# A hybrid attention and convolution block: one more large buffer and two fewer small ones, convolution operands in pairs of token halves, and earlier loads for the attention merges

## The chip, the cores and the metric

The kernel runs on one core of a Trainium2 chip. The metric is the device time of one execution in microseconds (us); the figure given for a kernel is the median of its timed runs. Beside that there is one profiled execution, whose trace gives the time of every instruction and of every DMA.

## The reference, cut to what matters

The block takes x (1024 tokens, 1024 channels), and everything is float32. A matrix product is made on TensorE from high and low parts (`hi*a + hi*b + lo*a`), so each product costs three matmuls, and each operand has first to be split by ScalarE (the high part) and VectorE or GpSimd (the low part).

```python
h = rms_norm(x, g_pre_mix)
q, k, v, glu_in, z_ga, z_gc = split(h @ w_in)
# three head groups, dilation 1, 4 and 16; each gives an output o_g and a log denominator lse_g
alpha  = softmax(stack(lse_g), axis=groups)
y_attn = (sum_g alpha_g * o_g) @ w_attn_out              # the "merge", then "ao"
u      = depthwise_conv(u * sigmoid(gate)) + b_dw
y_conv = silu(layer_norm(u)) @ w_conv_out + b_conv_out    # "co"
merged = sigmoid(z_ga) * y_attn + sigmoid(z_gc) * y_conv
x = x + rms_norm(merged @ w_mix_out)                      # then the SwiGLU FFN
```

## The kernel before

The engines' instruction streams are written out by hand: each engine executes its instructions in the order in which the Python code emits them. Two clocks in that code set the order. `unit()` emits one product of 128 channels by 512 tokens: for each of 8 k-tiles three matmuls, then a `tick()`. A tick runs the steps that `later(n, step)` has put n ticks ahead, one piece of a weight split at every third tick, and one step of each background generator in `gens` (a generator that yields n skips n ticks). After each matmul, `beat()` advances the attention generator by `RATE` steps, so attention is woven into whatever product is running.

The stages that matter here, in order:

1. The value products `B.v(g, hg)` run with `conv_norm` in the background: it normalizes the convolution's output and, in its last loop, lets VectorE multiply (L1272) and ScalarE apply Silu (L1276), block after block. In the kernel before, ScalarE writes the result with even and odd tokens brought into their natural places (a stride of two elements) and itself starts the store to DRAM (L1278).
2. Attention starts in the second of these products and goes on through the rest of them, through `plain_gate` (the late gate) and the first products of the convolution's output projection. For each head pair and group it loads queries and keys by `stack_load` (L872 to L879, DMAs of 64 rows each), the bias tile (L483) and the values (L900 to L905). `att_s` makes the scores, `att_e` the exponentials (L1066), `att_t` transposes them (L1091, split at L1098 and L1099), and `att_p` multiplies by the values (L1126) and copies the result to an output tile (L1145) that is stored in `d_att`. A step's `att_t` comes three steps after its exponentials, its `att_p` one step after its `att_t`.
3. `conv_split` loads the Silu results from `d_act` half a block at a time (L1292) and splits them (L1222 on ScalarE, L1223 on VectorE) into the operands of the projection.
4. The projection runs over (n, hf) in the order (0,0), (1,0), (0,1), (1,1), (2,0), (2,1) and so on; n is the column of weights `co[n]` (loaded at L177, split at L188 and L189) and hf the half of the tokens. VectorE takes a finished product out of PSUM and multiplies it by its gate (L1557); gates are loaded at L1540 and stored at L1559.
5. `merge(hp)` combines the three groups of a head pair: it computes the weights alpha in a small tile (L1170 to L1177), writes them to `d_w` (L1180), and, after attention has ended (`self.fine is None`) and its turn has come, loads each group's output (L1190) and its weights spread over 64 partitions twice (`spread`, L1158), multiplies and adds on VectorE (L1197, L1201, L1205, L1209, L1212), and splits the result. The merges of head pairs 0 and 1 have their weights ready long before attention ends.

All DMAs but the Silu stores, and a few at the start, are started by SyncE (SP) and go to one queue. Large buffers (`slot`, 128 x 1024) number 41, small ones (`half`, 128 x 512) 13; PSUM in the attention stage is divided into two banks each for products (`g`), scores (`s`), transposes (`t`) and outputs (`o`), and is divided anew for products (`g=6, s=2`) once attention has ended.

Of the kernel before, what the change touches and what calls it, by code (L numbers as in the profile page):

```python
# [46 lines left out]
NSLOT = 41  # L47

NRING = 3
NHALF = 13  # L50
# [12 lines left out]
class Build:  # L63
# [135 lines left out]
    def quarters(self, i, c):  # L199


        nc = self.nc
        if c == 0:
            self.hl[i] = {}
        o = self.hl[i]
        r1, r2 = self.raw[i - 1], self.raw[i]
        a11, a12, a21, a22 = r1[:, :H], r1[:, H:], r2[:, :H], r2[:, H:]
        add = self.wsplit.tensor_tensor
        l, r = slice(0, H), slice(H, 2 * H)
        if c == 0:  # L210
            h, w = self.both(r1)
            o["A11"], o["A12"] = (h[:, l], w[:, l]), (h[:, r], w[:, r])
        elif c == 1:
            self.s12 = self.ring()
            add(self.s12[:, l], a21, a22, op=OP.add)
            add(self.s12[:, r], self.s12[:, l], a11, op=OP.add)  # L216
        elif c == 2:
            h, w = self.both(self.s12)
            o["S1"], o["S2"] = (h[:, l], w[:, l]), (h[:, r], w[:, r])
        elif c == 3:  # L220
            self.s34 = self.half(), self.half()
            add(self.s34[0], a11, a21, op=OP.add)
            add(self.s34[1], self.s12[:, r], a12, op=OP.add)
            self.s12 = None
        elif c == 4:
            h, w = self.slot(F32R), self.slot(F32R)
            for n, s in ("S3", l), ("S4", r):
                x = self.s34[n == "S4"]
                nc.scalar.copy(h[:, s], x)
                add(w[:, s], x, f(h[:, s]), op=OP.subtract)  # L230
                o[n] = (h[:, s], w[:, s])
            self.s34 = x = None
        else:
            x, y = self.half(F32R), self.half(F32R)
            nc.scalar.copy(x, a22)
            add(y, a22, f(x), op=OP.subtract)
            o["A22"] = (x, y)
            del self.raw[i], self.raw[i - 1], self.hl[i]
# [863 lines left out]
    def att_p(self, live, k):  # L1102
# [33 lines left out]
        O = self.O  # L1136
        if g == 0:
            d = O[:, u * 128:u * 128 + 256]
        elif g == 1:
            d = O.rearrange("p (t c) -> p c t", c=4)[:, u // 2]  # L1140
        else:
            d = O.rearrange("p (m c) -> p c m", c=8)[:, u:u + 2]
        for h in range(2):
            x = ps[0:64, h * 256:(h + 1) * 256]
            nc.vector.tensor_copy(d[h * 64:(h + 1) * 64], x if g < 2 else x.rearrange("p (c m) -> p c m", c=2))  # L1145
# [16 lines left out]
    def merge(self, hp, st):  # L1162
# [33 lines left out]
        yield 8  # L1196
        nc.vector.tensor_tensor(y, y, x, op=OP.mult)  # L1197
# [14 lines left out]
        nc.vector.tensor_tensor(y, y, w, op=OP.add)  # L1212
        w = None
        yield 2
        self.OT[hp] = self.both(y)

    turn = 0
# [12 lines left out]
    def conv_norm(self):  # L1230
# [39 lines left out]
        for b in range(9):  # L1270
            if b < 8:
                nc.vector.tensor_tensor(A[b], A[b], rs, op=OP.mult)  # L1272
            if b:
                a, A[b - 1] = A[b - 1], None
                o = self.slot()
                nc.scalar.activation(o.rearrange("p (m e) -> p e m", e=2), a.rearrange("p (e m) -> p e m", e=2),  # L1276
                                     AF.Silu, bias=self.col(C_BLN + b - 1), scale=self.col(C_GLN + b - 1))
                nc.scalar.dma_start(self.d_act[b - 1], o)  # L1278
# [6 lines left out]
    def conv_split(self):  # L1285
        self.cop = [[], []]
        nc = self.nc

        def load(i):
            hf, b = divmod(i, 8)  # L1290
            x = self.half()
            nc.sync.dma_start(x, self.d_act[b][:, hf * H:(hf + 1) * H])  # L1292
# [82 lines left out]
def build(ctx, tc, aps):  # L1375
# [81 lines left out]
    def plain_gate(n, job, early):  # L1457
        w = B.weights(job)
# [12 lines left out]
        if not early:  # L1471
            nc.sync.dma_start(B.d_gc[n], s)
# [39 lines left out]
    for i, (g, hg) in enumerate(vj):  # L1512
# [15 lines left out]
    def conv_rhs(hf):  # L1528
        def at(kt):
            while len(B.cop[hf]) <= kt:  # L1530
                next(cs[0])
# [6 lines left out]
    def gate_load(d):  # L1538
        c = B.slot()
        nc.sync.dma_start(c, d)  # L1540
# [21 lines left out]
    B.finish(cs)  # L1562
# [443 lines left out]
```

## Time and profile before

| | us |
|---|---|
| median of 3 runs | 1735.37 |
| lowest, highest run | 1732.92, 1735.95 |
| profiled execution, its own time | 1730.98 |
| its span in the trace | 1729.2 |

The profiled execution took 1.8 us more than its span, and 4.4 us less than the median. The trace has 24623 instructions; the granted TensorE clock was 0.996 on average. In what follows PE is TensorE, PEld its weight loads, DVE VectorE, ACT ScalarE, POOL GpSimd and SP SyncE; a q behind an engine's name means its sequencer, such as a DMA start. Times of day are us from the start of the span.

### The profile page before, as it was taken

The numbers are of one execution on the slowest core, as the hardware profiler recorded it, in microseconds if no ns is written. First come the engines' busy times: TensorE is split into PE (matmuls) and PEld (weight loads), VectorE is DVE, ScalarE is ACT, GpSimd is POOL, SyncE is SP. The second block draws the span as 40 slices with busy tenths as digits, with TensorE's granted clock in tenths as the row PEclk, the third lists the DMA queues.
The fourth block names the chain that finished last, engine by engine and source line by source line (L and its number), as shares of the span: only waits on it lengthen the run. The fifth ranks groups of instructions, "written<-read, shape, count | busy, mean of one in ns | idle before, by whom it ended". The sixth has DMA issues, their size and how long they took to land.

```text
span 1729.2 us, 24623 instructions
## 1 busy us (share of the span) xinstructions
PE 1698.1 (98%) x8754; PEld 1441.0 (83%) x8754; DVE 1255.7 (73%) x2235; ACT 793.6 (46%) x1589; POOL 466.9 (27%) x387
## 2 busy tenths in 40 slices
PE   8999999999999989999998999999999999999998
PEld 7788888888888989999886888888888888888786
DVE  6789978888997566777955855676556655677586
ACT  6344444344444476676612345743333333354463
POOL 0017778887885233433200120000000000000000
PEclk9999999999999999999999999999999999999999
DMA  4352434455678697879699731223322322494234
GB/s 164 109 175 87 158 116 141 163 180 168 183 181 217 183 282 206 243 200 229 208 278 322 268 129 62 104 74 122 116 91 92 121 99 92 149 372 148 84 136 153
DMA packets 170872, 285.53 MB, mean 165 GB/s; under 512 B 55506, under 2 KB 86733, under 8 KB 170749
## 3 DMA queue, kind: packets, MB, share of 16 engines
q1 hardware_dynamic: 169196, 279.26, 51.1%
q10 hardware_dynamic: 1440, 4.46, 0.7%
q8 instruction: 69, 1.13, 0.3%
q14 instruction: 55, 0.44, 0.1%
q0 software_dynamic: 112, 0.24, 0.0%
HBM read 192.15 MB, written 96.47 MB: 167 GB/s over the span
## 4 chain that ended last, share of the span: by engine, by line
PE 89%; DMA 5%; ACT 2%; DVE 2%; issue 1%; SPq 1%; POOL 0%; ACTq 0%; DVEq 0%; POOLq 0%
PE p L326 16%; PE p L325 16%; PE p L327 16%; PE p L1890 12%; PE p L1619 4%; PE p L309 3%; PE p L311 3%; PE p L313 3%; PE p L1126 3%; PE p L1053 2%; PE p L950 2%; PE p L952 2%; PE p L954 2%; PE p L560 2%; DMA b<-dw 2%; PE p L1091 2%
## 5 line engine op out<-in xcount | busy, mean ns | idle before, releaser
L325 PE MATMUL p<-b,b 128*128 128x512 f32 x1032 | 401.6, 389 | 0.0
L327 PE MATMUL p<-b,b 128*128 128x512 f32 x1032 | 401.5, 389 | 0.0
L326 PE MATMUL p<-b,b 128*128 128x512 f32 x1032 | 401.5, 389 | 0.0
L325 PEld LDWEIGHTS p<-b,b 128*128 128x128 f32 x1032 | 193.7, 188 | 41.1 <-ACT c L339 0.6
L327 PEld LDWEIGHTS p<-b,b 128*128 128x128 f32 x1032 | 193.7, 188 | 40.1
L326 PEld LDWEIGHTS p<-b,b 128*128 128x128 f32 x1032 | 193.7, 188 | 40.1
L1890 PE MATMUL p<-b,b 128*128 128x512 f32 x924 | 210.2, 389 | 0.9 <-ACT b L1222 0.7
L1890 PEld LDWEIGHTS p<-b,b 128*128 128x128 f32 x924 | 173.4, 188 | 37.6 <-ACT b L1222 1.1
L690 DVE SCALAR_TENSOR_TENSOR p<-b,par,p 128x511 f32<-128x511 f32 (+14 forms) x232 | 163.3, 738 | 0.0
L313 PE MATMUL p<-b,b 128*128 128x512 f32 x368 | 147.1, 400 | 9.1 <-DVE b L189 9.1
L309 PE MATMUL p<-b,b 128*128 128x512 f32 x368 | 147.5, 401 | 0.0
L311 PE MATMUL p<-b,b 128*128 128x512 f32 x368 | 146.6, 398 | 0.0
L195 ACT CAST b<-d 128x1024 fp32r<-128x1024 f32 x86 | 90.4, 1051 | 108.3 <-POOL d L216 58.2
L196 POOL TENSOR_TENSOR b<-d,b 128x1024 fp32r<-128x1024 f32 x44 | 106.9, 2429 | 101.6 <-ACT b L195 88.5
L196 DVE TENSOR_TENSOR b<-d,b 128x1024 fp32r<-128x1024 f32 x42 | 51.3, 1221 | 105.1 <-ACT b L195 105.1
L950 PE MATMUL p<-b,b 128*128 128x256 f32 x384 | 113.4, 295 | 2.4 <-ACT d L965 2.4
L954 PE MATMUL p<-b,b 128*128 128x256 f32 x384 | 112.5, 293 | 0.0
L952 PE MATMUL p<-b,b 128*128 128x256 f32 x384 | 112.4, 293 | 0.0
L1223 DVE TENSOR_TENSOR b<-c,b 128x512 fp32r<-128x512 f32 x101 | 70.9, 702 | 41.6 <-ACT b L1222 40.8
L1222 ACT CAST b<-c 128x512 fp32r<-128x512 f32 x101 | 62.5, 618 | 67.2 <-PE p L1890 22.5
L1223 DVE TENSOR_TENSOR b<-b,b 128x512 fp32r<-128x512 f32 x117 | 79.9, 687 | 18.3 <-ACT b L1222 16.6
L1066 ACT ACTIVATE c<-c,stat 128x128 f32<-128x128 f32 (+1 forms) x192 | 84.9, 445 | 12.3 <-DVE stat L1056 11.6
(234 smaller groups left out, 3349.5 us busy)
## 6 DMA issues: line engine op xcount, KB each, us to landing
b<-w_in SPq DMA_DIRECT2D x30, 512.0 KB, 5.2
dk<-c SPq DMA_DIRECT2D x48, 256.0 KB, 2.9
dq<-c SPq DMA_DIRECT2D x48, 256.0 KB, 3.6
b<-dq SPq DMA_DIRECT2D x48, 256.0 KB, 4.7
b<-dk SPq DMA_DIRECT2D x48, 256.0 KB, 6.7
b<-w_fi SPq DMA_DIRECT2D x24, 512.0 KB, 4.9
d<-w_in SPq DMA_DIRECT2D x23, 512.0 KB, 4.5
dqS<-c SPq DMA_DIRECT2D x44, 256.0 KB, 2.1
```

The source lines that it names most:

```text
L196: self.wsplit.tensor_tensor(lo, x, f(hi), op=OP.subtract)
L309: nc.tensor.matmul(ps, hi[:, s], a, start=kt == 0, stop=False)
L311: nc.tensor.matmul(ps, hi[:, s], b, start=False, stop=False)
L313: nc.tensor.matmul(ps, lo[:, s], a, start=False, stop=kt == nk - 1)
L325: nc.tensor.matmul(ps, hi[:, s], a, start=first and kt == 0, stop=False, skip_group_check=True)
L326: nc.tensor.matmul(ps, hi[:, s], b, start=False, stop=False, skip_group_check=True)
L327: nc.tensor.matmul(ps, lo[:, s], a, start=False, stop=kt == 3, skip_group_check=True)
L690: nc.vector.scalar_tensor_tensor(A[i][:, j:], src[i][:, :H - j], w[i], A[i][:, j:], op0=OP.mult, op1=OP.add)
L950: nc.tensor.matmul(o, a, hi[:, s], start=kt == 0, stop=False)
L954: nc.tensor.matmul(o, b, hi[:, s], start=False, stop=kt == KT - 1)
L1223: nc.vector.tensor_tensor(s[:, 512:512 + n], src, f(s[:, :n]), op=OP.subtract)
L1890: nc.tensor.matmul(acc[t], x, y, start=first and e == 0, stop=last and e == 2, skip_group_check=True)
```

## The change

- **Buffers.** `NSLOT` 41 becomes 42, `NHALF` 13 becomes 11. In `quarters`, which prepares weights for the products by seven multiplications, the sums S3 and S4 and the split of A22 move from two small buffers each to one large one each, and the split of S3 and S4 is one instruction each on ScalarE and GpSimd instead of two.
- **Convolution operands.** `conv_norm` writes the Silu results with even tokens first and odd tokens behind, without a stride, and their stores are started by SP five ticks later instead of by ScalarE at once. `conv_split` loads two halves into one large buffer, keeps two pairs, starts 16 ticks later than before, and splits with other gaps. The half hf of the projection is now the even or the odd tokens, and the gate is read and written with a stride of two.
- **Merges.** The attention outputs are laid out so that alpha can be written to `d_w` in rows of 128 numbers (six rows of 8 x 128 tokens): the weights go through a transpose on TensorE and a copy on ScalarE first. A merge may load its first two groups as soon as the projection has begun (`self.hH is None`) and it is at most one turn ahead; only its multiplications wait for the end of attention. PSUM is divided anew once all four merges have their weights (`weighed == 4`).
- **DMAs put off.** The store of an attention output comes three ticks after its last copy instead of one; the late gate's store, the first gate load and the first column of projection weights are issued some ticks later, the second column with the first product of the projection.

The core of the diff:

```diff
-NSLOT = 41
+NSLOT = 42
-NHALF = 13
+NHALF = 11
...
         elif c == 4:
-            h, w = self.slot(F32R), self.slot(F32R)
-            for n, s in ("S3", l), ("S4", r):
...
+            h, w = self.both(self.s34)
+            o["S3"], o["S4"] = (h[:, l], w[:, l]), (h[:, r], w[:, r])
...
-            x, y = self.half(F32R), self.half(F32R)
+            x = self.slot(F32R)
...
-            self.later(1, lambda x=self.O: nc.sync.dma_start(self.d_att[g, hp], x))
+            self.later(3, lambda x=self.O: nc.sync.dma_start(self.d_att[g, hp], x))
...
         yield 1
-        nc.sync.dma_start(self.d_w[hp].rearrange("f (p u) -> p f u", u=8),
-                          t[:, 80:].rearrange("p (f u) -> p f u", u=8))
-        t = m = r = w = low = tot = None
-        yield 6
-
-        while self.fine is not None or hp > self.turn:
+        m = r = w = low = tot = None
+        yield 3
+        ps = self.bank("t")
+        nc.tensor.transpose(ps[0:48, :128], t[:, 80:], self.ident)
+        nc.scalar.copy(t[0:48], ps[0:48, :128])
+        ps = None
+        self.weighed += 1
+        yield 1
+        nc.sync.dma_start(self.d_w[hp].rearrange("f (u p) -> (f u) p", u=8), t[0:48])
+        t = None
+        yield 4
+
+        while self.hH is not None or hp > self.turn + 1:
             yield 0
...
         z, w = load(1), self.spread(hp, 1)
         yield 8
+        while self.fine is not None or hp > self.turn:
+            yield 0
         nc.vector.tensor_tensor(y, y, x, op=OP.mult)
...
-                nc.scalar.activation(o.rearrange("p (m e) -> p e m", e=2), a.rearrange("p (e m) -> p e m", e=2),
-                                     AF.Silu, bias=self.col(C_BLN + b - 1), scale=self.col(C_GLN + b - 1))
-                nc.scalar.dma_start(self.d_act[b - 1], o)
+                nc.scalar.activation(o, a, AF.Silu, bias=self.col(C_BLN + b - 1), scale=self.col(C_GLN + b - 1))
+                self.later(5, lambda b=b, o=o: nc.sync.dma_start(self.d_act[b - 1], o))
...
-        x = [load(i) for i in range(3)]
-        yield 14
+        self.cn = 0
+        x = [load(), load()]
+        yield 16
         for i in range(16):
-            self.cop[i // 8].append(self.split(x.pop(0), H))
-            if i < 13:
-                x.append(load(i + 3))
-            yield 3 if i < 3 else 1 + i % 2
-            while i == 3 and not self.room:
+            while i > 3 and not self.room:
                 yield 0
+            self.cop[i // 8].append(self.split(x[0][:, i % 2 * H:(i % 2 + 1) * H], H))
+            if i % 2:
+                x.pop(0)
+                if self.cn < 16:
+                    x.append(load())
+            yield 2 if i < 4 else 1 + i % 2
...
-        w = B.weights(job)
+        w = B.weights(job) if early else B.timed([job], co[:1], 3, 9)[0]
...
-            nc.sync.dma_start(B.d_gc[n], s)
+            B.later(4, lambda: nc.sync.dma_start(B.d_gc[n], s))
...
-            cs = B.bg(B.conv_split())
-            B.later(20, lambda: B.load_ahead(co[0]))
+            cs = []
+            B.later(16, lambda: cs.append(B.bg(B.conv_split())))
...
-    nxt = gate_load(B.d_gc[0])
+    nxt = gate_load(B.d_gc[0], 3)
...
-        if B.tags["g"] == 2 and B.fine is None:
+        if B.tags["g"] == 2 and B.weighed == 4:
             B.banks(g=6, s=2)
         ps = B.unit(ws[n], conv_rhs(hf), KT)
-        c = mg[n][:, hf * H:(hf + 1) * H]
+        c = mg[n].rearrange("p (m e) -> p e m", e=2)[:, hf]
```

More of the change, by code (lines that the diff above doesn't have):

```diff
@@ L220, in quarters @@
         elif c == 3:
[L221 to L223 removed]
+            self.s34 = self.slot()
+            add(self.s34[:, l], a11, a21, op=OP.add)
+            add(self.s34[:, r], self.s12[:, r], a12, op=OP.add)
             self.s12 = None
         elif c == 4:
[L226 to L237 removed]
+            h, w = self.both(self.s34)
+            o["S3"], o["S4"] = (h[:, l], w[:, l]), (h[:, r], w[:, r])
+            self.s34 = None
+        else:
+            x = self.slot(F32R)
+            nc.scalar.copy(x[:, l], a22)
+            add(x[:, r], a22, f(x[:, l]), op=OP.subtract)
+            o["A22"] = (x[:, l], x[:, r])
             del self.raw[i], self.raw[i - 1], self.hl[i]
@@ L1211, in merge @@
         yield 2
-        nc.vector.tensor_tensor(y, y, w, op=OP.add)
-        w = None
+        z = self.slot()
+        nc.vector.tensor_tensor(z.rearrange("p (m c) -> p c m", c=8), *(a.rearrange("p (c m) -> p c m", c=8) for a in (y, w)),
+                                op=OP.add)
+        y = w = None
         yield 2
-        self.OT[hp] = self.both(y)
-    turn = 0
+        self.OT[hp] = self.both(z)
+    turn = weighed = 0
     def split(self, src, n):
@@ L1275, in conv_norm @@
                 o = self.slot()
[L1276 to L1278 removed]
+                nc.scalar.activation(o, a, AF.Silu, bias=self.col(C_BLN + b - 1), scale=self.col(C_GLN + b - 1))
+                self.later(5, lambda b=b, o=o: nc.sync.dma_start(self.d_act[b - 1], o))
+                o = None
             yield 1
@@ L1287, in conv_split, with load @@
         nc = self.nc
[L1289 to L1292, printed above, removed]
-            return x
-        x = [load(i) for i in range(3)]
-        yield 14
+        def load():
+            x = self.slot()
+            for e in range(2):
+                hf, b = divmod(self.cn + e, 8)
+                nc.sync.dma_start(x[:, e * H:(e + 1) * H], self.d_act[b][:, hf * H:(hf + 1) * H])
+            self.cn += 2
+            return x
+        self.cn = 0
+        x = [load(), load()]
+        yield 16
         for i in range(16):
-            self.cop[i // 8].append(self.split(x.pop(0), H))
-            if i < 13:
-                x.append(load(i + 3))
-            yield 3 if i < 3 else 1 + i % 2
-            while i == 3 and not self.room:
-                yield 0
+            while i > 3 and not self.room:
+                yield 0
+            self.cop[i // 8].append(self.split(x[0][:, i % 2 * H:(i % 2 + 1) * H], H))
[4 more added lines that the diff above has]
+            yield 2 if i < 4 else 1 + i % 2
     def rstd_rows(self, m, e):
@@ L1536, in build, with gate_load @@
     mg = {}
-    def gate_load(d):
+    def gate_load(d, late=0):
         c = B.slot()
-        nc.sync.dma_start(c, d)
+        if late:
+            B.later(late, lambda: nc.sync.dma_start(c, d))
+        else:
+            nc.sync.dma_start(c, d)
         return c
-    nxt = gate_load(B.d_gc[0])
+    nxt = gate_load(B.d_gc[0], 3)
     ws = {}
```

13 lines of the change are left out of this document (7 added, 6 removed).

## The prediction

> **What bounds the kernel now.** I read the page first, then TensorE's waits, then a table by stages.
>
> ```profile
> PE 1698.1 (98%) x8754; PEld 1441.0 (83%) x8754; DVE 1255.7 (73%) x2235; ACT 793.6 (46%) x1589; POOL 466.9 (27%) x387
> ```
>
> PE is busy for 98% of the span, so a change that leaves the products alone can only win the places where PE waits. The list of its waits (us in total, times, longest) names them:
>
> ```profile
> PE p L313 <- DVE b L189: 9.1, 3, 4.8
> ...
> PE p L950 <- ACT d L965: 2.4, 2, 1.5
> PE p L1053 <- DVE stat L1056: 2.4, 1, 2.4
> PE p L1053 <- DMA b<-dk: 1.3, 1, 1.3
> ```
>
> Three places: about 600 to 620, where ScalarE is late (4.8 us); one wait for keys (1.3); and the projection, where PE waits for a weight split on VectorE (9.1). The stage table (stretch, length, busy of PE, PEld, DVE, ACT and POOL, granted clock, DMA share, GB/s) shows the last of them and what the DMA engines do before it:
>
> ```profile
> 600.00:620.00 20.00, 15.22 (x123) 14.61 (x122) 13.13 (x16) 15.23 (x15) 9.37 (x7) 1.00 0.73 269
> 820.00:847.00 27.00, 25.70 (x188) 21.82 (x187) 23.80 (x74) 20.33 (x70) 9.64 (x13) 1.00 1.02 315
> 847.00:868.00 21.00, 20.63 (x145) 16.70 (x144) 18.48 (x53) 10.38 (x37) 2.77 (x4) 1.00 0.14 43
> 868.00:902.00 34.00, 33.70 (x149) 27.57 (x147) 18.54 (x26) 4.10 (x7) 0.00 (x0) 1.00 1.00 304
> 902.00:940.00 38.00, 29.19 (x113) 23.27 (x114) 23.89 (x26) 8.02 (x12) 0.00 (x0) 0.91 1.03 320
> ```
>
> The DMA queue is full from 820 to 847 (share 1.02), idle for 21 us (0.14) while attention ends, and full again while the merges run. From 902 on the waits also lower the clock to 0.91, which costs 38 x 0.09 = 3.4 us. So the projection loses 9.1 + 3.4 = 12.5 us. The change moves four of the merges' twelve group loads, with their weights, in front of that idle stretch.
>
> **Part 1, the Silu stores (600 to 620).** ScalarE's timeline (start, length, operation, idle time before it):
>
> ```profile
> 610.46 1.34 ACT L1276 ACTIVATE b<-b,par 128x1024 f32<-128x1024 f32 x1 [0.46 <-ACT b L1276]
> 611.83 0.33 ACTq L1278 DMA_DIRECT2D dact<-b  x1
> 612.20 1.30 ACT L1276 ACTIVATE b<-b,par 128x1024 f32<-128x1024 f32 x1 [0.40 <-DVE b L1272]
> 613.54 0.33 ACTq L1278 DMA_DIRECT2D dact<-b  x1
> 613.96 0.59 ACT L965 COPY d<-p 128x512 f32<-128x512 f32 x1 [0.45 <-ACT b L1276]
> ```
>
> Each store started by ScalarE leaves it idle for 0.40 to 0.46 us; eight make 3.4 us, all ahead of the copies (L965) that PE waits for. The strided write may cost up to 0.28 us more each: 1.30 to 1.34 against 1.06 for the same size without a stride or a parameter column, so between 0 and 2.2 us in all.
>
> ```profile
> L1257 ACT ACTIVATE b<-b 128x1024 f32<-128x1024 f32 x8 | 8.3, 1059 | 0.0
> ```
>
> Both go, and ScalarE finishes 3.4 to 5.6 us sooner. The second wait for L965 (1.5) and the score wait behind it (2.4) vanish; of the first, 0.9 of the 2.4, only the DMA's 0.3 goes, since there PE's own product came late. Gain 4.2 us. SP, which takes the stores over, only queues them; they are read 100 ticks later.
>
> **Part 2, the tail of attention (825 to 868).** This is what SP starts as the projection begins, in order:
>
> ```profile
> 825.98 0.33 SPq L1472 DMA_DIRECT2D dgc<-b  x1
> 826.36 0.42 SPq L1540 DMA_DIRECT2D b<-dgc  x1
> 826.83 1.03 SPq L177 DMA_DIRECT2D b<-w_co  x1
> 827.90 0.49 SPq L1540 DMA_DIRECT2D b<-dgc  x1
> 828.43 1.15 SPq L879 DMA_DIRECT2D b<-dk  x2
> 829.92 0.33 SPq L1292 DMA_DIRECT2D c<-dact  x1
> 830.36 0.38 SPq L483 DMA_DIRECT2D c<-rep  x1
> 831.52 0.32 SPq L905 DMA_DIRECT2D b<-dv  x1
> ```
>
> The condition `hH is None` holds from here. The first tick of product (0,0) falls between the keys (dk) and the bias tile (rep); in it merges 0 and 1 each issue one group and its spread weights, and two ticks later, ahead of the values (dv), each the other. The queue serves in order, and these rows give its speeds:
>
> ```profile
> 829.00:834.00 5.00, 5.00 (x38) 4.26 (x37) 3.75 (x14) 3.77 (x15) 4.63 (x7) 1.00 1.03 411
> 834.00:839.00 5.00, 3.78 (x29) 3.05 (x27) 4.79 (x15) 2.73 (x9) 2.58 (x4) 1.00 1.06 235
> ```
>
> From 829 to 834 it moves the four 512 KB tiles on 128 partitions, at 411 GB/s, 1.3 us each; then mostly keys on 64 partitions, at 235, 2.2 us per 512 KB. `spread` writes 64 partitions at a time too, so a group with its weights takes 3.5 us. [...]
>
> The keys now come 1.3 us sooner (the late gate's store and a gate load move behind, one column of weights is added), which ends the 1.3 us wait. Then two groups, 7.0 us, stand ahead of the bias tile; it lands 5.7 us later. Its user in the kernel before is the third row here:
>
> ```profile
> 839.07 0.41 PE L1053 MATMUL p<-b,b 128*128 128x128 f32 x2 [1.29 <-DMA b<-dk]
> 839.26 0.74 DVE L1557 SCALAR_TENSOR_TENSOR b<-p,par,b 128x512 f32<-128x512 f32 x1
> 840.37 0.29 DVE L1056 CUSTOM_DVE_ANT_0 c<-p,c 128x128 f32<-128x128 f32 x1 [0.36 <-DMA c<-rep]
> 843.55 0.62 ACT L1222 CAST b<-c 128x512 fp32r<-128x512 f32 x1 [0.67 <-DMA c<-dact]
> 845.63 0.62 ACT L919 CAST b<-b 128x512 fp32r<-128x512 f32 x1
> 851.76 0.74 DVE L1557 SCALAR_TENSOR_TENSOR b<-p,par,b 128x512 f32<-128x512 f32 x1
> ```
>
> VectorE already waits for it, so it stands until about 846, with the low parts of the transposes (L1099) queued behind. The operand pair of the projection fares worse. The one that is split between the fourth and fifth row above, at 844.5, is loaded eight ticks before. Ahead of it in the queue now, from 832.7: keys 2.2, two groups 7.0, bias 1.1, gate load 1.3, two groups 7.0, values 1.3, gate store 1.3, itself 1.3; it ends at 855.2. Keys that left the queue near 836.2 released PE at 839.07, so 2.8 us pass to the release: 858. ScalarE stands at L1222 from 844.5 to 858, 13.5 us, with the exponentials behind. PE needs a step's copies one step later; 8 ticks took 12.5 us (the products taken out at 839.26 and 851.76), a step 1.6 ticks, so 2.5 us are covered and PE loses 11. The new gaps also put the last two halves' splits in the ticks that use them, three later than before; ScalarE's 0.62 and VectorE's subtraction then stand in PE's way, about 2 us (bounds 0 and 4). Loss 13 us, with the key wait in it. Bounds: 3 (only the bias tile's 5.7 less 2.5 of cover) to 17. Transfers that lie beyond 858 find the old idle stretch.
>
> **Part 3, the projection (868 to 940).** VectorE's timeline before:
>
> ```profile
> 879.74 1.22 DVE L1201 TENSOR_TENSOR b<-b,b 128x1024 f32<-128x1024 f32 x1 [2.53 <-DMA b<-dw]
> 888.60 1.23 DVE L1209 TENSOR_TENSOR b<-b,b 128x1024 f32<-128x1024 f32 x1 [4.52 <-DMA b<-datt]
> 898.60 1.23 DVE L1201 TENSOR_TENSOR b<-b,b 128x1024 f32<-128x1024 f32 x1 [3.72 <-DMA b<-dw]
> 915.80 1.22 DVE L1201 TENSOR_TENSOR b<-b,b 128x1024 f32<-128x1024 f32 x1 [4.21 <-DMA b<-dw]
> 917.60 0.68 DVE L189 TENSOR_TENSOR b<-b,b 128x512 fp32r<-128x512 f32 x1
> ```
>
> Its multiplications wait for merges' loads, and the weight split L189, for which PE waits, stands behind. With two groups of merges 0 and 1 there, turns follow every 6 ticks instead of 17, so all four merges fall into about 50 ticks instead of 90: the remaining eight groups' worth of loads is asked for faster than the queue gives it. Counting the queue from attention's end at the speeds above (weights, gates and stores included), the third merge's last group ends after 31 us and is usable at 33; VectorE then has two multiplications, a sum and a gate ahead of the sixth column's split, ready at 39.7. PE, after six products of 24 matmuls, wants it at 33.8. With 1.5 us at the fifth column, that is 6 us of waits and some 1.5 of clock, 7.5 in place of 12.5. Gain 5 (bounds: 12.5 if nothing is late, -4 if the queue is a fifth slower).
>
> **Part 4, the small things.** Four transposes of alpha and their copies: 0.1 us of PE each by the row below, up to 0.5 with the bank. Longer `d_w` rows: the write of 768 pieces of 32 bytes lies in the second row, where the DMA share is 0.09, 0.4 us of the queue.
>
> ```profile
> L1356 PE MATMUL p<-ident,b 128*128 128x128 f32 x64 | 9.9, 274 | 1.2 <-ACT b L1348 1.0 <-ACT b L1362 0.2
> 860.00:864.00 4.00, 4.00 (x29) 3.11 (x28) 3.85 (x11) 0.75 (x2) 0.00 (x0) 1.00 0.09 6
> ```
>
> [...] Fewer small buffers: the operand loads that used them are gone, and nothing is late there (0; bound 2). One more large buffer takes the extra tile of the seven-product stages, where GpSimd's longer subtraction still has eight ticks (0; bound 3). Loss 0.4.
>
> **Sum.** -4.2 + 13 - 5 + 0.4 = +4.2 on the profiled 1730.98, 1735.2; on the median, 4.4 above the profiled run, 1739.6.
>
> **The rivals.**
> - *Faster: the early loads find the idle stretch.* If the loads of merges 0 and 1 cost the tail only the lower bound (3, the bias tile), and VectorE is then never late for a weight split (-12.5), the sum is -4.2 + 3 - 12.5 + 0.4 = -13, 1722. It decides at whether the operand pair lands by 847. For: 847 to 868 has room for all 14 us; against: order in the queue, not room, delays the pair. A half-way case (tail 8, projection -12.5) gives -8, 1727. Together 0.25.
> - *The loads are held back.* They need eight large buffers; if these come free only as the projection advances, SP issues late, the tail loses about 4 and the projection gains 3: -3, 1732. Chance 0.12. For: buffers are scarce; against: 16 are freed as the products on `hH` end.
> - *Even.* The tail loses 9: 0, 1735. Chance 0.13.
> - *Worse.* The queue is slower with spreads, tail 17, projection +4: +17, 1752. Chance 0.05.
>
> **How the numbers follow.** The forecast has 0.45, with a range of its own of 1735 to 1748. The range for all, 1724 to 1749, leaves out the ends of the first and last rival. A measurement can tell about 0.2% (3.5 us, 1731.9 to 1738.8). Faster: 0.25 + half of the held-back case, 0.31. Same: the other half, most of the even case, a little of the forecast, 0.21. Slower: 0.48.
>
> **What would show it.** Right: ScalarE with no gaps at L1276; an L1056 wait of about 6 us for the bias tile near 840; ScalarE idle some 8 us more before an operand cast (L1222) on dact; attention ending near 876 or later; merges' waits for dw closer together and one PE wait on L189 of 3 to 5 us. Wrong: attention ending by 866 with rep and dact unwaited for, which would mean that the queue does not serve in order or that the loads went elsewhere; or no L189 wait in the projection.

## The result, and the profile after

| | before | after |
|---|---|---|
| median of the runs, us | 1733.47 (6 runs, 1732.92 to 1735.95) | 1739.49 (6 runs, 1737.50 to 1742.36) |
| profiled execution, own time, us | 1730.98 | 1742.27 |
| its span, us | 1729.2 | 1740.5 |

The ratio is 1.0033, 95% interval 1.0020 to 1.0046: slower by a little. The forecast was 1739.6. The two profiled executions lie 11.3 us apart and not 6, since one lies 2.5 us below its median and the other 2.8 above; the balance below is made of the two traces.

The page of after gives the engines' shares; PE is busy 6 us longer than before (1704.0 against 1698.1) for the same products and four small transposes:

```profile
PE 1704.0 (98%) x8758; PEld 1446.5 (83%) x8758; DVE 1255.2 (72%) x2214; ACT 790.3 (45%) x1550; POOL 465.7 (27%) x365
```

The list of PE's waits of after (us in total, times, longest):

```profile
PE p L1122 <- DVE c L1095: 8.7, 2, 8.2
...
PE p L1122 <- ACT c L1094: 4.3, 1, 4.3
PE p L1049 <- DMA b<-dk: 3.4, 2, 2.7
PE p L309 <- DVE b L189: 3.4, 2, 3.0
PE p L1180 <- DVE mrg L1174: 1.4, 1, 1.4
PE p L305 <- ACT b L1231: 1.0, 1, 1.0
PE p L307 <- DVE b L1232: 0.8, 1, 0.8
```

Lines have moved: L1122 multiplies by the values, L1094 and L1095 split the transposes, L1049 makes the scores, L1231 and L1232 split the projection's operands. The waits around 610 (4.8 us, for ScalarE's copies and for the scores behind them) are gone; the wait for the weight split (L189) fell from 9.1 to 3.4; the waits at the tail of attention are new (8.7, 4.3, and 1.8 at L305 and L307), and so are one for keys (3.4) and one of 1.4 at L1180, where alpha's transposition waits for VectorE. The stage table of after (stretch, length, busy of PE, PEld, DVE, ACT, POOL, granted clock, DMA share, GB/s):

```profile
600.00:620.00 20.00, 20.00 (x167) 19.87 (x167) 15.88 (x29) 17.83 (x30) 9.24 (x7) 1.00 0.72 250
620.00:640.00 20.00, 16.37 (x122) 15.64 (x121) 11.03 (x32) 10.62 (x35) 4.88 (x8) 0.83 1.07 280
820.00:847.00 27.00, 22.38 (x163) 18.95 (x160) 17.73 (x57) 17.15 (x56) 9.43 (x12) 0.97 1.01 269
847.00:868.00 21.00, 12.67 (x57) 10.07 (x57) 10.21 (x36) 8.48 (x30) 3.03 (x4) 0.66 0.95 284
...
902.00:940.00 38.00, 34.65 (x145) 27.90 (x144) 30.16 (x30) 10.85 (x15) 0.00 (x0) 0.96 0.93 299
```

From 847 to 868 the DMA engines are now busy (0.95 instead of 0.14): the queue does fill the idle stretch. But PE stands for 8 of those 21 us, and its clock is 0.66.

To follow the time I use marks in PE's timeline that every kernel has: the start of the products (0,0) and (2,0), of the first product of the attention's own output (ao), and the end. From (0,0) to (2,0) is the tail of attention; from (2,0) to ao is the rest of the projection.

| kernel | (0,0) starts | tail | projection | ao to end | median | ratio to before, 95% |
|---|---|---|---|---|---|---|
| before | 825.35 | 43.08 | 78.27 | 782.50 | 1733.47 | |
| after | 826.35 | 62.40 | 72.44 | 779.30 | 1739.49 | 1.0033 (1.0020 to 1.0046) |
| e1_late_loads | 824.18 | 43.53 | 77.77 | 779.28 | 1727.94 | 0.9969 (0.9957 to 0.9981) |
| e2_loads_plus15 | 824.84 | 43.50 | 73.92 | 779.29 | 1724.11 | 0.9951 (0.9933 to 0.9968) |
| e3_silu_on_before | 827.61 | 44.59 | 77.39 | 782.40 | 1736.14 | 1.0018 (1.0002 to 1.0033) |
| e4_early_on_before | 823.59 | 61.77 | 86.97 | 782.45 | 1756.21 | 1.0131 (1.0113 to 1.0150) |
| f1_buffers_on_before | 826.38 | 48.44 | 77.69 | 779.28 | 1734.84 | 0.9998 (0.9980 to 1.0016) |
| f2_stores_plus12 | 824.75 | 43.51 | 77.98 | 779.29 | 1721.77 | 0.9925 (0.9899 to 0.9951) |
| f3_gate_first | 824.49 | 61.68 | 72.48 | 779.30 | 1740.65 | 1.0033 (1.0016 to 1.0050) |
| f4_short_rows | 825.54 | 60.67 | 80.60 | 779.31 | 1748.69 | 1.0069 (1.0046 to 1.0093) |

Stage lengths are of the profiled execution, one for each kernel; medians and ratios are of the timed runs. One execution leaves a stage uncertain: the third value product (600 to 646 in before) takes 45.6 us in before, and 43.4 in e4 and 44.3 in g1 (below), whose instructions are the same up to there; e2 and f2, alike in the projection, differ in it by 4.1 us. Runs of before on the other chips had medians of 1733.4 to 1734.9. After against before, then: +1.0 up to (0,0), +19.3 in the tail, -5.8 in the projection, -3.2 from ao to the end, 11.3 in all.

How the tail loses 19.3 us stands in two rows, of before and of after:

```profile
825.35:868.43 43.08, 41.41 (x294) 34.31 (x293) 38.34 (x113) 27.25 (x93) 12.41 (x16) 1.00 0.58 187
```

```profile
826.35:888.75 62.40, 47.64 (x296) 38.58 (x294) 35.86 (x115) 28.22 (x95) 12.46 (x16) 0.86 0.72 209
```

PE's idle time grew from 1.67 to 14.76 us, by 13.1. The other 6.2 us are the same 294 to 296 matmuls at a lower clock, 47.64 us instead of 41.41. SP's queue in after, and the three waits that follow from it (SP's starts; then VectorE's, ScalarE's and PE's timelines, with the idle time before each in brackets):

```profile
828.46 0.33 SPq L1194 DMA_DIRECT2D b<-datt  x1
...
832.11 3.10 SPq L1155 DMA_DIRECT2D b<-dw  x2
835.72 0.38 SPq L479 DMA_DIRECT2D c<-rep  x1
836.86 0.69 SPq L1556 DMA_DIRECT2D b<-dgc  x1
...
846.89 0.53 SPq L901 DMA_DIRECT2D b<-dv  x1
...
853.64 2.29 SPq L1302 DMA_DIRECT2D b<-dact  x2
```

```profile
849.07 0.75 DVE L1575 SCALAR_TENSOR_TENSOR b<-p,par,b 128x512 f32<-128x512 f32 x1 [9.65 <-DMA b<-dgc]
...
850.06 0.40 ACT L1062 ACTIVATE c<-c,stat 128x128 f32<-128x128 f32 x1 [9.11 <-DVE stat L1052]
...
850.62 0.37 PE L1122 MATMUL p<-c,b 128*66 128x128 f32 x1 [8.24 <-DVE c L1095]
...
860.90 0.62 ACT L1231 CAST b<-b 128x512 fp32r<-128x512 f32 x1 [6.62 <-DMA b<-dact]
...
861.84 0.34 PE L1122 MATMUL p<-c,b 128*66 128x128 f32 x2 [4.25 <-ACT c L1094]
```

Merge loads (datt, dw) stand ahead of the bias tile (rep), the gate (dgc), the values and the operand pair (dact), as in the prediction's list. The gate holds VectorE until 849.07, and the pair holds ScalarE until 860.90; PE stops behind both. SP itself now takes 3.10 us to start two spreads (1.08 for the two before them), and starts the pair only at 853.64. The chain of work that ended last (start, length, what) passes through the spreads to the pair:

```profile
829.51 12.05 DMA b<-dw
841.58 11.99 DMA b<-dw
853.64 7.18 DMA b<-dact
```

### The profile page after: what moved, and what is told of

Its sections match the earlier page's. It is cut to its first block, busy times and chain, and to the rows that moved or that the text cites. A ratio compares the mean times of both kernels' runs of the same rounds, so it can differ in the third digit from the quotient of the medians.

```text
span 1740.5 us, 24527 instructions
## 1 busy us (share of the span) xinstructions
PE 1704.0 (98%) x8758; PEld 1446.5 (83%) x8758; DVE 1255.2 (72%) x2214; ACT 790.3 (45%) x1550; POOL 465.7 (27%) x365
## 4 chain that ended last, share of the span: by engine, by line
PE 92%; DMA 4%; DVE 2%; ACT 1%; POOL 1%; issue 1%; SPq 0%; DVEq 0%; ACTq 0%; POOLq 0%
PE p L321 15%; PE p L323 15%; PE p L322 15%; PE p L1908 12%; PE p L1637 5%; PE p L305 4%; PE p L309 4%; PE p L307 4%; PE p L1122 3%; PE p L946 2%; PE p L948 2%; PE p L950 2%; PE p L556 2%; PE p L1049 2%; PE p L1087 2%; DMA b<-dw 1%
## 5 line engine op out<-in xcount | busy, mean ns | idle before, releaser
L321 PE MATMUL p<-b,b 128*128 128x512 f32 x1204 | 468.6, 389 | 0.3 <-ACT c L340 0.3
L323 PE MATMUL p<-b,b 128*128 128x512 f32 x1204 | 468.4, 389 | 0.0
L322 PE MATMUL p<-b,b 128*128 128x512 f32 x1204 | 468.4, 389 | 0.0
L321 PEld LDWEIGHTS p<-b,b 128*128 128x128 f32 x1204 | 226.0, 188 | 47.8 <-ACT c L340 0.7
L323 PEld LDWEIGHTS p<-b,b 128*128 128x128 f32 x1204 | 226.0, 188 | 47.1
L322 PEld LDWEIGHTS p<-b,b 128*128 128x128 f32 x1204 | 226.0, 188 | 46.9
L1908 PE MATMUL p<-b,b 128*128 128x512 f32 x924 | 209.6, 389 | 0.0
L1908 PEld LDWEIGHTS p<-b,b 128*128 128x128 f32 x924 | 173.4, 188 | 36.0
L309 PE MATMUL p<-b,b 128*128 128x512 f32 x368 | 147.9, 402 | 3.4 <-DVE b L189 3.4
L305 PE MATMUL p<-b,b 128*128 128x512 f32 x368 | 148.3, 403 | 1.0 <-ACT b L1231 1.0
L307 PE MATMUL p<-b,b 128*128 128x512 f32 x368 | 147.1, 400 | 0.8 <-DVE b L1232 0.8
L1232 DVE TENSOR_TENSOR b<-b,b 128x512 fp32r<-128x512 f32 x133 | 91.5, 692 | 28.8 <-ACT b L1231 26.7
L1231 ACT CAST b<-b 128x512 fp32r<-128x512 f32 x133 | 82.2, 620 | 53.2 <-PE p L1908 18.1
L1122 PE MATMUL p<-c,b 128*66 128x128 f32 (+1 forms) x620 | 87.6, 244 | 13.1 <-DVE c L1095 8.7
```

What stands on the lines that cost most here:

```text
L305: nc.tensor.matmul(ps, hi[:, s], a, start=kt == 0, stop=False)
L307: nc.tensor.matmul(ps, hi[:, s], b, start=False, stop=False)
L309: nc.tensor.matmul(ps, lo[:, s], a, start=False, stop=kt == nk - 1)
L321: nc.tensor.matmul(ps, hi[:, s], a, start=first and kt == 0, stop=False, skip_group_check=True)
L322: nc.tensor.matmul(ps, hi[:, s], b, start=False, stop=False, skip_group_check=True)
L323: nc.tensor.matmul(ps, lo[:, s], a, start=False, stop=kt == 3, skip_group_check=True)
```

## Experiments

**Which part owns the tail's loss?** First the changed kernel with the loads put back to their old time:

```diff
-        while self.hH is not None or hp > self.turn + 1:
+        while self.fine is not None or hp > self.turn:
```

> The changed kernel with one condition put back: a merge's loads wait, as in the kernel before, until the last attention half is done. Everything else of the change stays. Theory (the early loads crowd SP's queue in the tail of attention): the way from the first product of the projection, (0,0), to the fifth, (2,0), which took 43.1 us before (825.35 to 868.43) and 62.4 us after (826.35 to 888.75), comes back to 43 to 47 us; the projection's gain of 5.8 us goes with it; the total lands at 1731 to 1736 us. Rival (the tail was lost by the paired operands, the two halves split late, the gate load put off by 3 ticks or the smaller stock of small buffers): the tail keeps at least 10 of its 19.3 us, and with the projection's gain gone the total is 1740 to 1746 us.

Measured: tail 43.53, projection 77.77, total 1727.94. The whole loss of the tail is that of the early loads; without them, pairs, late splits and the late gate load cost it 0.5 us. The projection's gain goes with them. And what is left is faster than before, by 0.3%, below the range of both theories: 3.2 us of it lie behind ao (see f1). PE's waits in the projection:

```profile
PE p L309 <- DVE b L189: 9.3, 2, 6.7
```

Then the early loads alone, on the kernel before (the same condition, and the wait for `fine` ahead of the multiplications):

> The kernel before with one part of the change alone: the first two groups of merges 0 and 1 are loaded as soon as the last products on hH are through, not when the last attention half is done. Operands stay single, the gate load stays where it was. Theory (the loads crowd the tail): (0,0) to (2,0) takes 51 to 60 us instead of 43.1, the projection (2,0) to the output's start gains 3 to 6 us, and the total rises by 5 to 12 us. Rival (the loss belongs to the pairing, the late splits or the late gate load): the tail grows by 3 us at most and the total falls by 0 to 4 us.

Measured: tail 61.77, as in after and a little above the 60 that I had allowed. But the projection takes 86.97 us, 8.7 longer than before, where I expected it 3 to 6 shorter; the total is up by 1.3%. PE waits for the weight split longer than ever (15.8 us):

```profile
PE p L313 <- DVE b L189: 15.8, 2, 8.5
PE p L1126 <- DVE c L1099: 8.8, 2, 8.5
PE p L1126 <- ACT c L1098: 4.9, 1, 4.9
```

So the tail's half of the theory holds, and the projection's gain needs something else of the change (see f4).

**Is it the amount of data or the order in the queue?** The changed kernel with the early loads let go 15 ticks after the projection's start, behind the bias tile, the gate, the values and the operand pairs:

```diff
-        while self.hH is not None or hp > self.turn + 1:
+        while not self.open or hp > self.turn + 1:
...
     B.hH = B.hL = None
+    B.later(15, lambda: setattr(B, "open", True))
```

> The changed kernel with the early loads of merges 0 and 1 opened 15 ticks after the start of the projection, so that the bias tile, the first gate load, the values and the first operand pairs stand ahead of them in SP's queue, and the loads fall into the stretch in which the kernel before left the DMA idle (860 to 864: share 0.09). Theory (order in the queue costs the tail, not the amount of data): (0,0) to (2,0) takes 43 to 48 us instead of 62.4, the projection's gain of 5 to 6 us stays, and the total is 1724 to 1732 us, below both kernels. Rival (the tail is lost by the other edits): 55 us or more, 1736 to 1741 us.

Measured: tail 43.50, projection 73.92 (it keeps 4.4 of the 5.8 us), total 1724.11, 0.5% below before. The tail's row (compare the two above):

```profile
824.84:868.34 43.50, 41.69 (x296) 34.27 (x295) 35.55 (x115) 28.16 (x95) 12.79 (x16) 1.00 1.02 298
```

The DMA engines are full throughout (1.02 instead of 0.72 in after), as much is moved as in after (298 GB/s for 43.5 us and 209 GB/s for 62.4 us both make 13.0 MB), and PE stands for 1.8 us only. Order, not amount, cost the 19 us.

**The gate load.** The prediction had not named the wait for the gate. The changed kernel with that load at its old place, ahead of the merges' loads:

```diff
-    nxt = gate_load(B.d_gc[0], 3)
+    nxt = gate_load(B.d_gc[0])
```

> The changed kernel with the first gate load of the projection started at once, not 3 ticks later, so that it stands ahead of the merges' early loads in SP's queue. Theory (the unnamed wait: VectorE stood 9.6 us at the gate product with the transposes' low parts queued behind, and PE 8.2 us behind those): that wait goes, but the bias tile and the operand pair still stand behind the loads, so (0,0) to (2,0) takes 52 to 58 us instead of 62.4 and the total is 1730 to 1736 us. Rival (the gate load was no later than the bias tile anyway): 60 us or more, the total within 2 us of the changed kernel.

Measured: tail 61.68, total 1740.65; the rival holds. VectorE now waits for the bias tile instead:

```profile
845.67 0.29 DVE L1052 CUSTOM_DVE_ANT_0 c<-p,c 128x128 f32<-128x128 f32 x1 [6.63 <-DMA c<-rep]
```

That is the prediction's own step ("stands until about 846"). The 3 us that VectorE wins are lost again, since the operand pair sets the end: PE's wait for L1094 grows from 4.3 to 5.1, and the clock is 0.83 instead of 0.86 over the tail.

**The stores of Silu.** On the kernel before, Silu without the stride, its stores by SP five ticks later, and the gate read with a stride:

```diff
-                nc.scalar.activation(o.rearrange("p (m e) -> p e m", e=2), a.rearrange("p (e m) -> p e m", e=2),
-                                     AF.Silu, ...)
-                nc.scalar.dma_start(self.d_act[b - 1], o)
+                nc.scalar.activation(o, a, AF.Silu, ...)
+                self.later(5, lambda b=b, o=o: nc.sync.dma_start(self.d_act[b - 1], o))
```

> The kernel before with one part of the change alone: Silu writes without a stride, its eight 512 KB stores are queued on SP five ticks later instead of being started by ScalarE, and the gate product reads the even and odd tokens with a stride. Theory (the stores' place in SP's queue): ScalarE's gaps of 0.40 to 0.46 us go and with them the waits of PE on the copies, 4.8 us in all, but the stores now stand ahead of the first keys of the next attention half in SP's queue, and PE waits 3 to 8 us for keys near 630 us; net -1 to +2 us. Rival (the forecast's part 1): no wait for keys, -4.2 us.

Measured: no gain; +0.2%, at the edge of what can be told. PE's waits from 600 to 645:

```profile
PE p L1053 <- DMA b<-dk: 2.8, 2, 2.0
PE p L950 <- ACT d L965: 1.8, 1, 1.8
PE p L1053 <- DVE stat L1056: 1.2, 1, 1.2
```

The waits of 4.8 us shrink to 3.0, and 2.8 us for keys come in their place. The third value product takes 47.7 us here, against 45.6 in before (43.4 and 44.3 with the same code in e4 and g1). In the changed kernel the old waits vanish wholly, the one for keys is 3.4 us, and the product takes 45.7 (44.8 in e1, 45.2 in e2).

To see whether the stores hold the keys up, the kernel of e2 with the stores twelve ticks after Silu instead of five (`self.later(12, ...)`), so that some stand behind the keys:

> The kernel with the early loads opened 15 ticks after the projection's start, and besides the eight stores of Silu started twelve ticks after their Silu instead of five, so that some of them stand behind the first keys in SP's queue. Theory (DMA is busy without a pause from 612 to 640, and keys wait behind 4 MB of stores): PE's waits for keys near 630, 3.9 us, fall to under 2 us, and the whole takes 2 to 4 us less than with the loads moved alone (1720 to 1722 us). Rival (buffers held longer make the queries' loads wait on SP): the waits stay or grow, 0 to +3 us.

Measured: the wait for keys is gone and the third value product takes 44.4 us (45.2 in e2). In its place PE waits once for VectorE, which I had not expected:

```profile
PE p L1122 <- DVE c L1095: 3.7, 1, 3.7
```

The median, 1721.77, is the lowest of all, 0.75% below before and about 1.1% below after. The step from e2 to f2 (0.9951 to 0.9925) is within their intervals, and the 0.8 us in the product no more than kernels with the same code differ by, so whether it gains by itself is not settled.

**The buffers.** On the kernel before, `NSLOT` 42, `NHALF` 11 and the quarters S3, S4 and A22 in large tiles:

> The kernel before with one part of the change alone: 42 large and 11 small buffers, and the quarters S3, S4 and A22 of the seven-product stages kept in one large tile each instead of two small ones (S3 and S4 then split by one operation of 1024 elements instead of two of 512). The forecast put this part at 0. Theory (from the traces of the first runs): it owns the 3.2 us by which all kernels with the whole change are shorter between the last merge product (1081.21 before) and the end, and it lightens ScalarE around 612 to 618, so that part of the 6.3 us of waits there goes; total -3 to -5 us. Rival: 0, within 1 us, and the 3.2 us belong to another part.

Measured: the theory is right on the stage behind ao (779.28, as in all kernels of the table with this part, against 782.4 to 782.5 in all without it) and wrong on the total, which stays the same (0.9998). What PE waited for there in the kernel before, and no longer does, is 1.9 of the 3.2 us:

```profile
PE p L1356 <- ACT b L1348: 1.0, 1, 1.0
PE p L1890 <- ACT b L1222: 0.7, 1, 0.7
PE p L1890 <- DVE b L1223: 0.2, 1, 0.2
```

The 3.2 us are given back: the last value product takes 58.0 us instead of 54.8, and PE waits 3.1 us for keys in the tail, 1.3 before:

```profile
PE p L309 <- DVE b L189: 8.3, 3, 3.9
PE p L1049 <- DMA b<-dk: 3.1, 1, 3.1
```

The likely cause is that operands are still loaded singly into small buffers, of which two are gone: from 740 to 870 SP stands 32 us ahead of these loads, 24 in before, with all later loads behind. In e1, with pairs (which need no small buffers) and the rest of the change, the gain stays; buffers and pairs alone were not run together.

**The rows of `d_w`.** The changed kernel with the weights written as before, in 768 pieces of 32 bytes, without the transpose, and with the old order of the attention outputs:

> The changed kernel with one part put back: a merge's weights are written to DRAM in 768 pieces of 32 bytes, without the transpose, and the attention output keeps its old order in memory. Early loads, pairs and buffers stay. The early loads alone cost the kernel before 8.7 us in the projection, while the whole change gains 5.8 there; what makes the difference is open. Theory (the long rows): the way from (2,0) to the first output product, 72.4 us after, goes to 78 us or more, and the total rises by 5 to 15 us. Rival (the forecast's 0.4 us; the difference lies with the pairs or the buffers): 71 to 74 us, the total within 2 us of the changed kernel.

Measured: projection 80.60 instead of 72.44, total 1748.69. The part that the prediction put at 0.4 us of the queue is worth 8.2 us of the projection once loads are early, and 9.2 us of the median. Part of how is seen in SP's own waits from 886 to 935, in f4 and in after:

```profile
SPq L1154 <- DMA dw<-mrg: 5.4, 1, 5.4
```

```profile
SPq L1155 <- DMA dw<-mrg: 2.4, 1, 2.4
```

A spread can't start before the weights have landed in DRAM. SP stands there, and all later loads behind it, 5.4 us instead of 2.4. Over the projection the queue also moves less in the time in which it is busy: 258 GB/s at a share of 0.84 in f4 against 290 at 0.88 in after:

```profile
886.21:966.81 80.60, 69.76 (x290) 56.73 (x288) 44.09 (x54) 14.48 (x23) 0.74 (x1) 0.92 0.84 258
```

```profile
888.75:961.19 72.44, 67.74 (x290) 54.98 (x289) 46.87 (x54) 14.49 (x24) 0.74 (x1) 0.98 0.88 290
```

Which of the two, pieces or order in memory, makes it slower was not separated, nor what makes up the other 6.4 us of e4's projection.

**The price of a spread.** Four kernels were meant to make the spreads cheaper, by one copy onto 128 partitions instead of two onto 64: on before, on after, on f2, and on f2 with each key tile's two copies (onto 64 partitions each) joined in the same way.

```diff
-        for e in range(2):
-            self.nc.sync.dma_start(x[e * 64:(e + 1) * 64], bass.AP(
-                tensor=d.tensor, offset=d.offset + (2 * g + e) * T, ap=[[0, 64], [1, T]]))
+        self.nc.sync.dma_start(x, bass.AP(
+            tensor=d.tensor, offset=d.offset + 2 * g * T, ap=[[T, 2], [0, 64], [1, T]]))
```

> The kernel before with one edit that the change doesn't contain: the two copies that spread a merge's weights, each onto 64 partitions, are one copy onto all 128. Theory (the projection is bound by the DMA queue, and a copy onto 64 partitions moves at 235 GB/s where one onto 128 moves at 411): each of twelve spreads takes 1.3 us instead of 2.2, 11 us of queue in all, so PE's waits for the weight split in the projection, some 9 us, fall to 0 to 4 us and the total falls by 4 to 9 us. Rival (the number of partitions is not what makes these copies slow, but that 64 partitions read the same row): the copies take as long as before, total within 2 us.

> The changed kernel as it is, with the spreads as one copy onto 128 partitions. It tests the size of the tail's loss: four spreads stand ahead of the operand pair and each is 0.9 us shorter. Theory (order in one queue, each transfer at its own rate): (0,0) to (2,0) shrinks from 62.4 by 3 to 6 us (3.6 us of queue and what the clock gives back), the projection by 3 to 6 us as well, total 1728 to 1734 us. Rival (the tail's loss is set by the time at which the loads are issued, or spreads onto 128 partitions are no faster): 61 us or more, total 1737 to 1741 us.

> The changed kernel with the early loads 15 ticks after the projection's start, Silu's stores 12 ticks after their Silu, and the spreads as one copy onto 128 partitions. Theory (bound by the queue): the projection from (2,0) to the first output product, 73.9 us with the loads moved alone, takes 66 to 70 us, where PE's own products need about 65; total 1714 to 1719 us. Rival (same row, not partitions): 73 to 78 us, 1720 to 1724 us.

> The same as the kernel with wide spreads, and besides the keys' tiles loaded by one copy onto 128 partitions each instead of two onto 64. Theory: keys land sooner in the stretch from 612 to 640, where DMA is busy without a pause; what is left of PE's wait there (3.7 us for VectorE at 635) shrinks, total 1 to 4 us below the kernel with wide spreads alone. Rival (PE waits there for queries or VectorE's own work): no change.

Measured: 1830.48, 1829.14, 1819.38 and 1983.14 us (ratios 1.0555, 1.0543, 1.0486 and 1.1428, each interval within 0.0025). All four theories and their rivals missed. A stretch of g1 with one spread alone in the queue:

```profile
877.00:880.00 3.00, 3.00 (x15) 2.46 (x15) 0.00 (x0) 0.00 (x0) 0.00 (x0) 1.00 0.13 52
```

It runs at 52 GB/s with a DMA share of 0.13, as much as two of 16 engines (0.13 x 16 = 2.1): 10.1 us for 512 KB. The copy's leading dimension is 2; whether that makes it slow was not shown. In g4 the keys' copies have the same shape, and PE waits 74 us for keys; the median is 163.8 us above that of g2, which has the other edits of g4. Since the new copies differ from the old in more than the number of partitions, these runs say nothing of what 64 partitions cost. They do test the price of order: each spread became 10.1 - 2.2 = 7.9 us longer, if the prediction's 2.2, read off the keys, holds for spreads. In after four of them stand ahead of the operand pair, 31.6 us, and the tail grew from 62.40 to 92.72, by 30.3. In before twelve are read during the projection, 95 us, and it grew from 78.27 to 175.74, by 97.5. In both places a longer transfer reaches PE almost one for one; the medians, with twelve longer spreads each, grew by 89.7 us (g5 against after) and 97.0 us (g1 against before). The clock is in these figures: over the execution it was 0.968 in both, against 0.991 in after and 0.996 in before. SP itself is held as well: one start takes 11.47 us in g1.

## Why the prediction was right in the sum, and where it was not

- **Part 1, the Silu stores (forecast -4.2, measured about 0).** The step that failed is "SP, which takes the stores over, only queues them". ScalarE did end its last Silu 3.3 us sooner (614.2 instead of 617.5; gaps of 0.3 to 0.9 us stay, for VectorE's multiplications), and PE's waits on it are gone. But from 612 to 640 the DMA engines are busy without a pause (share 1.05), and the 4 MB of stores now stand in SP's own queue ahead of the first keys, so PE comes sooner to a wait for keys (3.4 us, with the clock at 0.83 from 620 to 640 against 0.91); with half of the stores behind the keys this wait is gone (f2). The 4.8 us to be won were also partly chance: e4 and g1, with the same code there, wait 3.6 and 3.9. I had asked who reads the stores, and not what else is in the queue behind them.
- **Part 2, the tail (forecast +13, measured +19.3).** The mechanism was right: order in one queue, shown by e1, e2, e4 and g5 (tails of 43.53, 43.50, 61.77 and 92.72 us). So was the sum of the waits: PE's idle time grew by 13.1 us; VectorE was free of the bias tile at 845.67 (f3) for "about 846"; ScalarE got the pair at 860.90 for 858; the last halves' splits cost 1.8 for 2. The term left out is the clock: 6.2 us. I had read the clock's fall off the projection's row and not applied it to the waits that I was adding. The gate load, put off by three ticks into the merges' loads, was a wait that I had missed. With it, PE's 11 us behind the pair became 8.2 behind the gate and 4.3 behind the pair; f3, without it, has 5.6 behind the bias tile and 5.1 behind the pair, and nearly the same tail.
- **Part 3, the projection (forecast -5, measured -5.8).** PE stood 9.1 us here in before and 4.7 in after: 3.4 for L189, where the sum had 6 and the list of signs 3 to 5, and 1.4 at L1180. The clock, 0.98 instead of 0.96, gives the rest. (The sum's 39.7 is not explained: 33 and the durations of the operations it lists, 2 x 1.22, 1.23, 0.74 and 0.68, make 38.1, which would leave some 4.3 us of waits.) And the reasoning was incomplete: e4 and f4 show that the early loads bring this gain only together with the new way to write and lay out the weights.
- **Part 4, the small things (forecast +0.4).** The buffers, put at 0 with only losses as bounds, gain 3.2 us behind ao; without the rest of the change as much is lost ahead of it (f1). The long rows, put at 0.4 us of the queue, are worth 8.2 us of the projection together with the new order of the outputs, an amount that stands within part 3's measured gain. The transposes, put at 0.1 us each (by the row's 9.9 us for 64 it is 0.15), brought the wait of 1.4 us.
- **The sum (forecast +4.2; +11.3 between the two traces, +6.0 between the medians).** Misses of +4.2 (part 1) and +6.3 (part 2) meet -0.8 (part 3) and -3.6 (the rest), and 1.0 us ahead of the projection. That the median came out 0.1 us from 1739.6 is luck: the forecast added 4.2 to the median of the first three runs, 1735.37, which was 1.9 above the median of all six, and the medians moved by 1.8 more than forecast. Inside the 4.2, errors of both signs cancel too. The direction is not luck, since the tail's loss outweighs all else.
- **The rival "the early loads find the idle stretch"** failed on the point it named: the pair did not land by 847. e2 is that rival made true by another order, and it gives 1724.

## What to carry to other kernels

A transfer moved ahead into an idle stretch paid here only when it was queued behind everything that is urgent before that stretch (tail +19.3 us ahead of it, in after, and +0.4 behind it, in e2); put it there by the tick at which it is issued, not by the first moment at which its data are ready. When a store or load changes its queue, list what stands behind it on the new one, and look at what the clock may add to every wait of several microseconds that you forecast (here 6.2 us to waits of 8.2 and 4.3 in after, and nothing to those of up to 3.6 in e2's projection). And cost the parts of a change together: here buffers without the rest gave nothing (f1, 0.9998), and early loads without the new weight rows lost in the very stage where they were to win (8.7 us in e4).

## What the runs showed of the hardware

The clock after a wait was dearer than I had expected. A finer table of after, around its two long waits:

```profile
842.00:846.00 4.00, 0.38 (x4) 0.14 (x2) 0.00 (x0) 0.00 (x0) 0.00 (x0) 0.91 1.05 256
846.00:850.00 4.00, 0.00 (x0) 0.00 (x0) 0.93 (x4) 0.00 (x0) 0.00 (x0) 0.50 1.06 286
850.00:854.00 4.00, 3.38 (x14) 2.90 (x15) 3.78 (x18) 2.24 (x10) 0.00 (x0) 0.50 1.02 234
854.00:858.00 4.00, 3.59 (x20) 2.57 (x19) 0.69 (x1) 0.28 (x1) 0.00 (x0) 0.81 1.04 317
858.00:862.00 4.00, 0.16 (x2) 0.16 (x2) 0.45 (x1) 1.10 (x3) 0.00 (x0) 1.00 1.07 371
862.00:866.00 4.00, 3.55 (x16) 2.93 (x16) 3.27 (x14) 3.04 (x11) 2.00 (x3) 0.55 0.96 357
866.00:870.00 4.00, 4.00 (x20) 3.29 (x20) 2.49 (x9) 1.88 (x9) 1.04 (x2) 0.60 0.13 40
```

PE stops at about 842.4; the clock is down to 0.50 by 846 and stays there until after 854, though PE works again from 850.6. It is back at 1.00 by 858, when the second wait is already under way, and the work after that one runs at 0.55 and 0.60. In rows of half a microsecond from 840 to 870 the clock reads 1.00 or 0.50, and something between only in the four rows in which it passes from one to the other:

```profile
845.00:845.50 0.50, 0.00 (x0) 0.00 (x0) 0.00 (x0) 0.00 (x0) 0.00 (x0) 0.80 1.12 350
...
855.50:856.00 0.50, 0.50 (x5) 0.40 (x4) 0.00 (x0) 0.00 (x0) 0.00 (x0) 0.96 1.08 294
...
862.00:862.50 0.50, 0.18 (x2) 0.03 (x1) 0.50 (x3) 0.50 (x2) 0.06 (x1) 0.86 0.84 320
...
869.00:869.50 0.50, 0.50 (x4) 0.45 (x4) 0.12 (x2) 0.00 (x0) 0.00 (x0) 0.81 0.00 0
```

If such a row is part at 1.00 and part at 0.50 (0.80 over 0.5 us is 0.2 us at 0.50), the clock fell 2.9 and 4.8 us after PE had stopped (842.4 and 857.6), and rose 4.9 and 7.4 us after it had begun again (850.6 and 861.8). The two waits, of 8.2 and 4.3 us, so cost 6.2 us more (47.64 us of PE's time over the tail, against 41.41 in before).

Not every wait costs that. e2 and f2 wait alike for the weight split in the projection (5.9 us, the longest 3.6, and 6.5, the longest 4.3), but only in f2 does the clock fall (0.93, against 1.00 in e2), and PE is busy 3.4 us longer with the same 290 matmuls; this is most of the 4.1 us by which their projections differ. First f2, then e2:

```profile
868.26:946.24 77.98, 70.09 (x290) 56.60 (x289) 46.89 (x54) 14.52 (x24) 0.74 (x1) 0.93 0.85 270
868.34:942.26 73.92, 66.70 (x290) 53.70 (x289) 46.87 (x54) 14.60 (x24) 0.74 (x1) 1.00 0.90 285
```

The spread as one copy onto 128 partitions, with a leading dimension of 2, ran at 52 GB/s and a DMA share of 0.13 (g1), against 235 GB/s and 1.06 in the stretch of before that moves mostly keys, by copies of 64 rows each. What in the copy's shape makes the difference was not separated.
